# The 32 decay columns of a linear attention, multiplied together with the attention's keys and values

## The chip, the cores and the metric

The kernel runs on one core of a Trainium2 chip. The metric is the device time of one execution in microseconds (us). TensorE multiplies, ScalarE and VectorE read the products out of PSUM, GpSimd (POOL in the profile) takes element-wise work, and SyncE (SP) issues the loads.

## The reference

Two transformer layers on 256 tokens with a context of 256 more (512 in all, width 1024), and then a second block with experts. In each layer one wide weight gives all branches their inputs:

```
(a_q, a_k, a_v, a_g, g_q, g_k, g_v, g_af, g_ab, g_g,
 s_u, s_v, s_g, m_a, m_g, m_s) = jnp.split(h @ p['w_in'], pts, axis=-1)
...
def log_decay(pa, a2, ab):
    z = (pa @ a2 + ab).astype(jnp.float32)
    return heads(jax.nn.log_sigmoid(z) / GLA_GATE_TEMP, GLA_DK)
...
q = rms_norm(pq.reshape(B, N, ATTN_HEADS, ATTN_HEAD_DIM), q_norm)
k = rms_norm(pk.reshape(B, N, ATTN_KV_HEADS, ATTN_HEAD_DIM), k_norm)
```

The attention's keys and values (a_k, a_v) are 256 columns. The linear attention's two decay inputs (g_af, g_ab) are 16 columns each, 32 in all; a small product with a2 widens them to 512 columns, whose log-sigmoid is summed along the tokens.

## The kernel before

Every product is made of three TensorE passes on operands split in two parts: high times high, low times high, high times low. A weight comes in units of 512 rows by 256 columns (tile raw); `split_unit` makes the high part on ScalarE (whi, L97) and the low part on VectorE (wlo, L98). There are three buffers each of raw, whi and wlo. `gemm_T` (L228 to L230) gives products with features on the partitions, `gemm_tok` (L263 to L265) with tokens on the partitions. Their results lie in four PSUM banks that are handed out in turn, two called gm and two called ou; a bank is free for the next product when ScalarE or VectorE has read the last of it. Transposes have two banks of their own (tag tr), the small decay products two others (tag sc).

`branches` calls, for layer 0 once with 512 tokens and for layer 1 twice with 256 tokens, first `gla_proj`, then `attn_kv`. In `gla_proj` come the linear attention's queries (gqps), then the decay columns (gaps, one `gemm_T` over a chunk of 128 columns, of which only 32 are used), copied to pg on ScalarE; four products zps with a2; on ScalarE Abs, Exp and Ln of them (lgt), on VectorE the scans (g); then keys (gkps) and values (gmt, L263 to L265). `attn_kv` multiplies keys and values, copies v, normalises and rotates each tile of 128 keys (`norm_rope`: sq on ScalarE, ms and rsq on VectorE, rs on GpSimd, q on VectorE, ktok on GpSimd), and transposes it (trk).

The order of the instructions on each engine is set by a list scheduler when the program is built, and each engine works through its own list in that order; what a program's text puts first is only an input to it. Layer 1's first half (tokens 0 to 255) also finishes layer 0: the transposes trh, with hTh on ScalarE, hmod on VectorE and hTl on either VectorE or GpSimd, make the context tokens of layer 1's input.

Of the kernel before, what the change touches and what calls it, by code (L numbers as in the profile page):

```python
# [10 lines left out]
F32 = mybir.dt.float32  # L11
# [3 lines left out]
AF = mybir.ActivationFunctionType  # L15
# [29 lines left out]
C_AQ, C_AK, C_AG, C_GQ, C_GK, C_GV = 0, 512, 768, 1280, 1536, 1792  # L45
C_GATE, C_GG, C_SU, C_SV, C_SG = 2304, 2336, 2848, 3360, 3872
# [29 lines left out]
class Builder:  # L76
# [416 lines left out]
        L["kl"] = self.akv.tile([128, 512], F32R, tag="kl", name="kl")  # L493
        L["v"] = self.akv.tile([128, 4, 128], F32, tag="v", name="v")

    def attn_kv(self, t0, t1):
        nc, a, L = self.nc, self.a, self.L
        kh, kl, v = L["kh"], L["kl"], L["v"]
        tts = range(t0 // 128, t1 // 128)
        g = self.gemm_tok(self.chunk(a["w_in"][self.li], C_AK), tts)  # L500
        for tt in tts:
            kt = self.att.tile([128, 512], F32, tag="att2k", name="ktok")[:, :128]
            nc.scalar.activation(v[:, tt], g[tt][:, 128:256], AF.Copy)
            self.norm_rope(g[tt][:, 0:128], 2, 1, tt, kt.rearrange("p (h e) -> p h e", e=64))
            ps = self.ptr.tile([128, 128], F32, tag="tr", name="trk")
            nc.tensor.transpose(ps, kt, self.ident)
            ts = slice(tt * 128, tt * 128 + 128)
            for h in range(2):
                pr, other = slice(64 * h, 64 * h + 64), slice(64 - 64 * h, 128 - 64 * h)
                nc.scalar.activation(kh[pr, h, ts], ps[pr], AF.Copy)  # L510
                nc.vector.tensor_tensor(kl[pr, ts], ps[pr], kh[pr, h, ts].bitcast(F32), op=OP.subtract)
                nc.gpsimd.tensor_copy(kh[other, h, ts], kh[pr, h, ts])
# [135 lines left out]
    def gla_proj(self, t0, t1):  # L648

        nc, a, L = self.nc, self.a, self.L  # L650
        w = a["w_in"][self.li]
        n = t1 - t0
        nq = min(t1, self.nx) - t0
        ts = slice(t0, t1)

        def product(c0, t1, name):
            if c0 not in self.early:
                return self.gemm_T(self.chunk(w, c0), t0, t1, name)
            return self.early.pop(c0)

        def keys():
            for j, ps in enumerate(product(C_GK, t1, "gkps")):
                nc.scalar.activation(L["gk"][:, j, ts], ps, AF.Copy)
            self.tick()

        keys_first = C_GK in self.early
        if nq > 0:
            for j, ps in enumerate(product(C_GQ, t0 + nq, "gqps")):
                nc.scalar.activation(L["gq"][:, j, t0:t0 + nq], ps, AF.Copy, scale=0.125)  # L669
            self.tick()  # L670
        if keys_first:
            keys()
        u = self.chunk(w, C_GATE, 128)
        ps = self.gemm_T(u, t0, t1, "gaps", 128)[0]
        pg = self.tmp.tile([32, 512], F32, tag="tmp", name="pg")[:, :n]
        nc.scalar.activation(pg, ps[:32], AF.Copy)

        logs = []
        for d in range(2):
            t = self.gla.tile([128, 2, 512], F32, tag=("acc", "qin")[d], name="lgt")[:, :, :n]  # L680
            for j in range(2):
                z = self.psc.tile([128, 512], F32, tag="sc", name="zps")[:, :n]
                nc.tensor.matmul(z, L["a2"][:, d * 256 + j * 128:d * 256 + j * 128 + 128], pg, start=True, stop=True)
                ab = L["vT"][:, 24 + 2 * d + j:25 + 2 * d + j]
                nc.scalar.activation(t[:, j], z, AF.Abs, bias=ab)
                nc.vector.tensor_scalar(L["bd"][d][:, j, ts], z, ab, 0.0, op0=OP.add, op1=OP.min)
            logs.append(t)
        for t in logs:
            nc.scalar.activation(t, t, AF.Exp, scale=-1.0)
        for t in logs:  # L690
            nc.scalar.activation(t, t, AF.Ln, bias=1.0)
        for d in range(2):
            b = L["bd"][d][:, :, ts]
            nc.gpsimd.tensor_tensor(b, b, logs[d], op=OP.subtract)
            for j in range(2):
                bj = b[:, j]
                if d == 0:
                    nc.vector.tensor_tensor_scan(bj, self.scan_f[:, :n], bj, 0.0, OP.mult, OP.add)
                else:
                    nc.vector.tensor_tensor_scan(bj[:, ::-1], self.scan_b[:, :n][:, ::-1], bj[:, ::-1], 0.0, OP.mult,  # L700
                                                 OP.add)
        if not keys_first:
            keys()
        tts = range(t0 // 128, t1 // 128)
        for c in range(2):
            g = self.gemm_tok(self.chunk(w, C_GV + 256 * c), tts)
            for tt in tts:
                nc.scalar.activation(L["gv"][:, tt, 256 * c:256 * c + 256], g[tt], AF.Copy)
            self.tick()
# [489 lines left out]
    def branches(self, spans):  # L1199
        with ExitStack() as inner:  # L1200
            self.gla = self.pool("gla", bufs=1, stack=inner, reuse_waits="tile")
            self.att = self.pool("att", bufs=2, stack=inner, reuse_waits="tile")
            self.gla_tiles()
            self.attn_tiles()
            self.alternate = True
            for t0, t1 in spans:
                if t0:
                    self.tick(len(self.pending))
                self.gla_proj(t0, t1)
                self.attn_kv(t0, t1)  # L1210
            self.attn_q()
            self.gla_gate()
            self.alternate = False
            self.sgu_tiles()
            self.gla_core()
            self.attn_gate()
            y = self.L["y_s"] = self.slot.tile([128, 2, 4, self.nx], F32R, tag=self.half, bufs=self.nhalf, name="ysg")
            self.nc.scalar.activation(y[:, 0, 0, 0:1], self.ones, AF.Copy)
            self.attn_core()
            self.sgu_proj()  # L1220
            self.sgu_core()
# [749 lines left out]
```

## Time and profile before

| | us |
|---|---|
| median of 3 runs | 1337.82 |
| lowest, highest | 1335.53, 1343.2 |
| the profiled execution | 1342.17 |
| its span | 1339.8 |
| TensorE busy | 1262.4 |
| VectorE, ScalarE, GpSimd busy | 724.2, 577.9, 334.9 |

The profiled execution took 2.4 us more than its span and 4.3 us more than the median. A busy TensorE in the profile includes modelled ends of its products, so that a short wait can lie inside a busy stretch; the distance between the starts of products tells more.

### The profile page before, as it was taken

Reading aid. Unit: us, or ns where it says so; the run is one execution under the profiler, and the core shown is the slowest. Engines: PE = TensorE matmul, PEld = TensorE weight load, DVE = VectorE, ACT = ScalarE, POOL = GpSimd, SP = SyncE. Lnnn points to the kernel's source line nnn. Section 1 sums busy time; section 2 is a strip of 40 time slices with the busy share of each in tenths; the row PEclk is TensorE's granted clock in tenths of the full one; section 3 lists DMA queues with packets and bytes.
Section 4 is the critical chain, followed back from the end, with each engine's and each line's share of the span. In section 5 each row is a group of like instructions: output and inputs, shape, how many; then the busy total and the mean of one; then the engine's idle time right before and its main releaser. Section 6 shows DMA issues by size and latency. Waiting matters only on the chain.

```text
span 1339.8 us, 22959 instructions
## 1 busy us (share of the span) xinstructions
PE 1262.4 (94%) x8819; PEld 977.2 (73%) x8819; DVE 724.2 (54%) x1428; ACT 577.9 (43%) x1115; POOL 334.9 (25%) x373
## 2 busy tenths in 40 slices
PE   6999999999999999999999999999899989999975
PEld 3789888777777766799989988799898675333311
DVE  2565585775443323378768877646878455111112
ACT  2463454455343222346776554545465333222201
POOL 2237645340001101242246545002124020000000
PEclk9999999999999999999999999999899799999998
DMA  9613222211124676545555546246498546999994
GB/s 320 188 53 110 74 58 79 65 48 48 48 75 132 188 252 221 173 149 167 152 149 157 138 116 186 67 126 193 123 327 252 187 174 257 409 408 409 408 409 185
DMA packets 182165, 243.89 MB, mean 182 GB/s; under 512 B 15284, under 2 KB 154780, under 8 KB 182048
## 3 DMA queue, kind: packets, MB, share of 16 engines
q1 hardware_dynamic: 182048, 242.35, 54.9%
q8 instruction: 71, 1.16, 0.4%
q14 instruction: 46, 0.38, 0.1%
HBM read 241.27 MB, written 1.05 MB: 181 GB/s over the span
## 4 chain that ended last, share of the span: by engine, by line
PE 65%; DMA 15%; DVE 8%; ACT 4%; issue 3%; POOL 2%; SPq 1%; ACTq 0%; DVEq 0%; POOLq 0%
DMA gu<-w_up 7%; PE mgps L228 5%; PE mgps L230 5%; PE mgps L229 5%; PE gmt L263 4%; PE gmt L264 4%; PE gmt L265 4%; PE gups L1737 3%; DVE wlo L98 2%; DMA dn<-w_down 2%; DMA raw<-w_in 2%; PE brps L228 2%; PE brps L229 2%; PE brps L230 2%; PE aops L631 2%
## 5 line engine op out<-in xcount | busy, mean ns | idle before, releaser
L98 DVE TENSOR_TENSOR wlo<-raw,whi 128x1024 fp32r<-128x1024 f32 (+1 forms) x202 | 253.5, 1261 | 156.7 <-ACT whi L97 153.8
L97 ACT ACTIVATE whi<-raw 128x1024 fp32r<-128x1024 f32 (+1 forms) x216 | 212.5, 993 | 199.3 <-PE mgps L229 41.8
L264 PE MATMUL gmt<-wlo,hTh 128*128 128x256 f32 x480 | 138.0, 288 | 2.5 <-DVE wlo L98 2.5
L263 PE MATMUL gmt<-whi,hTh 128*128 128x256 f32 x480 | 137.3, 287 | 2.1 <-DVE a L587 0.9
L265 PE MATMUL gmt<-whi,hTl 128*128 128x256 f32 x480 | 137.3, 286 | 0.0
L228 PE MATMUL mgps<-hTh,whi 128*128 128x512 f32 (+1 forms) x384 | 132.0, 345 | 0.0
L229 PE MATMUL mgps<-hTl,whi 128*128 128x512 f32 (+1 forms) x384 | 130.6, 340 | 0.0
L230 PE MATMUL mgps<-hTh,wlo 128*128 128x512 f32 (+1 forms) x384 | 130.4, 342 | 0.0
L957 POOL TENSOR_TENSOR msum<-msum,tanh 128x512 f32<-128x512 f32 (+1 forms) x32 | 36.8, 1154 | 329.7 <-DVE tanh L956 310.2
L1737 PE MATMUL gups<-gu,xw 128*64 128x512 f32 (+1 forms) x512 | 97.5, 603 | 8.4 <-DMA gu<-w_up 8.4
L264 PEld LDWEIGHTS gmt<-wlo,hTh 128*128 128x128 f32 x480 | 92.6, 193 | 5.9 <-DVE wlo L98 2.9
L263 PEld LDWEIGHTS gmt<-whi,hTh 128*128 128x128 f32 x480 | 92.5, 193 | 3.9 <-ACT g L669 1.1
L265 PEld LDWEIGHTS gmt<-whi,hTl 128*128 128x128 f32 x480 | 92.7, 193 | 2.3 <-issue 2.2
L228 PEld LDWEIGHTS mgps<-hTh,whi 128*128 128x128 f32 x384 | 72.6, 189 | 12.9 <-issue 5.0
L230 PEld LDWEIGHTS mgps<-hTh,wlo 128*128 128x128 f32 x384 | 72.5, 189 | 10.2 <-issue 2.5
L229 PEld LDWEIGHTS mgps<-hTl,whi 128*128 128x128 f32 x384 | 72.7, 189 | 9.0 <-issue 2.0
L1737 PEld LDWEIGHTS gups<-gu,xw 128*64 128x64 f32 (+1 forms) x512 | 25.3, 124 | 62.0 <-issue 60.0
L203 POOL TENSOR_TENSOR frs<-rsq,mhalf 128x1 f32<-128x1 f32 x2 | 1.1, 549 | 234.7 <-DVE frs L1911 234.7
L1769 DVE SCALAR_TENSOR_TENSOR eth<-eth,gups 128x256 f32<-128x256 f32 x12 | 5.1, 421 | 99.8 <-ACT eth L1768 99.8
L1792 PE MATMUL dnps<-dn,hm 128*64 128x512 f32 (+1 forms) x256 | 52.2, 599 | 6.2 <-DMA dn<-w_down 6.0
L264 PE MATMUL gmt<-wlo,mm 128*128 128x256 f32 x192 | 54.5, 285 | 0.6 <-DVE wlo L98 0.6
L263 PE MATMUL gmt<-whi,mm 128*128 128x256 f32 x192 | 54.1, 285 | 0.0
(559 smaller groups left out, 3109.2 us busy)
## 6 DMA issues: line engine op xcount, KB each, us to landing
raw<-w_in SPq DMA_DIRECT2D x132, 512.0 KB
gu<-w_gate SPq DMA_DIRECT2D x64, 512.0 KB
gu<-w_up SPq DMA_DIRECT2D x64, 512.0 KB
dn<-w_down SPq DMA_DIRECT2D x28, 1024.0 KB
adar<-w_ada SPq DMA_DIRECT2D x32, 512.0 KB
raw<-w_out SPq DMA_DIRECT2D x32, 512.0 KB
adaw<-w_ada SPq DMA_DIRECT2D x16, 512.0 KB
raw<-w_in SPq DMA_DIRECT2D x32, 256.0 KB
```

Of the source, the lines that this page charges most:

```text
L97: nc.scalar.activation(hi, x, AF.Copy)
L98: return (eng or nc.vector).tensor_tensor(lo, x, hi.bitcast(F32), op=OP.subtract).ins
L228: nc.tensor.matmul(ps, wh, xh, start=(u == 0 and k == 0), stop=False)
L229: nc.tensor.matmul(ps, wh, xl, start=False, stop=False)
L230: nc.tensor.matmul(ps, wl, xh, start=False, stop=(u == len(acts) - 1 and k == 3))
L263: nc.tensor.matmul(out[tt], xh, hi[:, j, :n], start=first, stop=False, skip_group_check=True)
L264: nc.tensor.matmul(out[tt], xh, lo[:, j, :n], start=False, stop=False, skip_group_check=True)
L265: nc.tensor.matmul(out[tt], xl, hi[:, j, :n], start=False, stop=last, skip_group_check=True)
L631: nc.tensor.matmul(ops[halves[g], r], v[:, keys[0] // 128 + k, 64 * g:64 * g + 64], pts[g][:, k], start=(k == 0), stop=(k == nkc - 1), ski ...
L957: nc.gpsimd.tensor_tensor(sums[c, j], sums[c, j], ts[j], op=OP.add)
L1737: mm = nc.tensor.matmul(u["ps"][pr], u["x"][:, k, pr], u["gu"][ei][k // 4][:, :, k % 4], start=(k == 0), stop=(k == 7), skip_group_check=T ...
L1792: mm = nc.tensor.matmul(ps[pr], hm[:, f, pr], dns[ei][:, f, 512 * hf:512 * hf + 512], start=(f == 0), stop=(f == 1), skip_group_check=True ...
```

## The change

The chunk of 128 decay columns is no longer loaded and multiplied by itself. A new function loads 288 columns, 256 of keys and values and 32 of decay, in three units of 384, 384 and 256 rows (864, 864 and 576 elements in a partition), and multiplies them as tokens by features into one bank for each tile of 128 tokens (kvps). ScalarE copies the 32 decay columns of each tile (gt), TensorE transposes them (trg), and ScalarE copies the result to pg. `attn_kv` no longer multiplies: it takes the same banks, and is called in `gla_proj` ahead of the decay's further work.

```
-    def attn_kv(self, t0, t1):
+    def keys_values_gate(self, tts):
+
+
+        nc, w = self.nc, self.a["w_in"][self.li]
+        out = {tt: self.bank([128, 512], "kvps")[:, :288] for tt in tts}
+        for k0 in range(0, 8, 3):
+            nk = min(3, 8 - k0)
+            raw, hi, lo = (t.rearrange("p a n -> p (a n)")[:, :288 * nk].rearrange("p (a n) -> p a n", n=288)
+                           for t in self.unit_tiles())
+            for cs, c0, n in ((slice(0, 256), C_AK, 256), (slice(256, 288), C_GATE, 32)):
+                nc.sync.dma_start(raw[:, :, cs], w[128 * k0:128 * (k0 + nk), c0:c0 + n].rearrange(
+                    "(a p) n -> p a n", p=128))
+            self.split_unit(hi, lo, raw)
+            for tt in tts:
+                ts = slice(tt * 128, tt * 128 + 128)
+                for j in range(nk):
+                    k = k0 + j
+                    xh, xl = self.hTh[:, k, ts], self.hTl[:, k, ts]
+                    nc.tensor.matmul(out[tt], xh, hi[:, j], start=(k == 0), stop=False)
+                    nc.tensor.matmul(out[tt], xh, lo[:, j], start=False, stop=False)
+                    nc.tensor.matmul(out[tt], xl, hi[:, j], start=False, stop=(k == 7))
+        return out
+
+    def attn_kv(self, tts, g):
         nc, a, L = self.nc, self.a, self.L
         kh, kl, v = L["kh"], L["kl"], L["v"]
-        tts = range(t0 // 128, t1 // 128)
-        g = self.gemm_tok(self.chunk(a["w_in"][self.li], C_AK), tts)
...
-        u = self.chunk(w, C_GATE, 128)
-        ps = self.gemm_T(u, t0, t1, "gaps", 128)[0]
+        tts = range(t0 // 128, t1 // 128)
+        g = self.keys_values_gate(tts)
+        gt = self.tmp.tile([128, 4, 32], F32, tag="tmp", name="gt")
+        tp = self.ptr.tile([128, 512], F32, tag="tr", name="trg")[:32, :n]
+        for i, tt in enumerate(tts):
+            nc.scalar.activation(gt[:, i], g[tt][:, 256:288], AF.Copy)
+            nc.tensor.transpose(tp[:, 128 * i:128 * i + 128], gt[:, i], self.ident)
         pg = self.tmp.tile([32, 512], F32, tag="tmp", name="pg")[:, :n]
-        nc.scalar.activation(pg, ps[:32], AF.Copy)
+        nc.scalar.activation(pg, tp, AF.Copy)
+        self.attn_kv(tts, g)
...
                 self.gla_proj(t0, t1)
-                self.attn_kv(t0, t1)
```

The scheduler's lists change with it. In layer 0, this stands on ScalarE before, where the decay columns' copy pg is made (whi are the splits of the next weights, br and sgr belong to another branch's constants):

```order
L97 ACTIVATE whi_613<-raw_612 128x1024
L97 ACTIVATE whi_721<-raw_720 128x1024
L676 ACTIVATE pg_576<-gaps_551 32x512
L377 ACTIVATE br_511<-wsum_513 1x512
L382 ACTIVATE sgr_521<-sgr_516 128x512
L685 ACTIVATE lgt_578<-zps_579,vT_136 128x512
```

And this stands there now:

```order
L97 ACTIVATE whi_801<-raw_800 128x1024
...
L699 ACTIVATE gt_660<-kvps_542 128x32
L524 ACTIVATE v_534<-kvps_542 128x128
L97 ACTIVATE whi_909<-raw_908 128x1024
L702 ACTIVATE pg_670<-trg_661 32x512
L560 ACTIVATE sq_674<-kvps_539 128x128
L712 ACTIVATE lgt_766<-zps_767,vT_136 128x512
```

Four copies gt and four copies v, one of each for a tile, and a split (whi_909) have come ahead of pg, and the normalisation (sq) has come between the decay's steps. On TensorE the same place reads now, from the last product of the 288 columns on (zps are the products with a2, gmt_806 is the first bank of the linear attention's values; it is the bank in which kvps_539 lay):

```order
L516 MATMUL kvps_542<-whi_630,hTl_108 128x288
L700 MATMUL trg_661<-ident_74,gt_660 32x128 x4
L710 MATMUL zps_767<-pg_670,a2_477 128x512
L710 MATMUL zps_771<-pg_670,a2_477 128x512
L710 MATMUL zps_776<-pg_670,a2_477 128x512
L263 MATMUL gmt_806<-whi_795,hTh_107 128x256
```

Before, 29 products of the values stood between gaps and the first zps there, and more between one zps and the next; none stand between kvps and the third zps now.

In layer 1's first half TensorE had this before around the first two decay products (gkps are the linear attention's keys):

```order
L230 MATMUL gkps_6245<-hTh_5329,wlo_6241 128x256
L683 MATMUL zps_6206<-pg_6203,a2_3751 128x256
L683 MATMUL zps_6210<-pg_6203,a2_3751 128x256
L228 MATMUL gkps_6246<-hTh_5329,whi_6234 128x256
L229 MATMUL gkps_6246<-hTl_5330,whi_6234 128x256
```

It has this now:

```order
L516 MATMUL kvps_6151<-whi_6203,hTl_5314 128x288
L700 MATMUL trg_6222<-ident_74,gt_6221 32x128 x2
L710 MATMUL zps_6282<-pg_6227,a2_3735 128x256
L710 MATMUL zps_6286<-pg_6227,a2_3735 128x256
L228 MATMUL gkps_6321<-hTh_5313,whi_6310 128x256
```

And ScalarE has this now, from the split that needs the buffer of the third unit of the 288 columns (whi_6385) on:

```order
L97 ACTIVATE whi_6385<-raw_6384 128x1024
L699 ACTIVATE gt_6221<-kvps_6150 128x32
L699 ACTIVATE gt_6221<-kvps_6151 128x32
L524 ACTIVATE v_6074<-kvps_6150 128x128
L524 ACTIVATE v_6074<-kvps_6151 128x128
L702 ACTIVATE pg_6227<-trg_6222 32x256
L560 ACTIVATE sq_6231<-kvps_6150 128x128
L476 ACTIVATE hTh_5313<-trh_6139,mb_3783,ms_3782 128x256
```

Between kvps and zps there were the first bank of keys and several transposes before; now there is nothing. gkps_6321 takes the bank of kvps_6150, so it follows that tile's normalisation, and on GpSimd hTl of the same trh stands ahead of that normalisation's rs.

## Rows read from the trace of the kernel before

**Rows 1.** The page's part 1, busy time of each engine.
```profile
PE 1262.4 (94%) x8819; PEld 977.2 (73%) x8819; DVE 724.2 (54%) x1428; ACT 577.9 (43%) x1115; POOL 334.9 (25%) x373
```

**Rows 2.** Waits of TensorE between 50 and 125 us: total, times, longest.
```profile
PE early L239 <- DVE hTl L481: 1.5, 1, 1.5
```

**Rows 3.** TensorE in layer 0: the decay columns' stage; then timeline (start, duration).
```profile
56.39:61.95 5.56, 5.56 (x24) 1.00 0.67 186
...
63.45 0.28 PE L265 MATMUL gmt<-whi,hTl 128*128 128x256 f32 x1
...
65.97 0.28 PE L265 MATMUL gmt<-whi,hTl 128*128 128x256 f32 x1
...
67.65 1.02 PE L683 MATMUL zps<-pg,a 32*128 32x512 f32 x2
```

**Rows 4.** Timeline of ScalarE in layer 0.
```profile
61.93 1.06 ACT L97 ACTIVATE whi<-raw 128x1024 fp32r<-128x1024 f32 x1 [1.61 <-PE gaps L229]
62.89 0.57 ACT L676 ACTIVATE pg<-gaps 32x512 f32<-32x512 f32 x1
...
68.71 0.69 ACT L685 ACTIVATE lgt<-zps,vT 128x512 f32<-128x512 f32 x1 [0.27 <-PE zps L683]
...
73.64 1.04 ACT L689 ACTIVATE lgt<-lgt 128x1024 f32<-128x1024 f32 x1
...
75.73 1.28 ACT L691 ACT_TABLE_LOAD   x1
77.03 1.06 ACT L691 ACTIVATE lgt<-lgt 128x1024 f32<-128x1024 f32 x1
```

**Rows 5.** Timelines of GpSimd and VectorE in layer 0, the decay's sums.
```profile
78.16 2.41 POOL L694 TENSOR_TENSOR g<-g,lgt 128x1024 f32<-128x1024 f32 x1 [25.92 <-ACT lgt L691]
...
80.60 2.34 DVE L698 TENSOR_TENSOR_SCAN g<-ku,g 128x512 f32<-128x512 uint8 x2 [0.61 <-POOL g L694]
82.86 0.67 DVE L741 TENSOR_TENSOR kh<-g 128x512 f32<-128x512 f32 x1
83.44 0.75 DVE L786 TENSOR_TENSOR qlv<-g 128x256 f32<-128x256 f32 x2
```

**Rows 6.** Timelines of GpSimd and VectorE in layer 0, a key tile's normalisation.
```profile
101.87 0.71 POOL L203 TENSOR_TENSOR rs<-rsq,mhalf 128x2 f32<-128x2 f32 x1 [6.77 <-DVE rsq L202]
...
102.61 0.29 DVE L546 TENSOR_TENSOR q<-gmt,rs 128x128 f32<-128x128 f32 x1 [0.82 <-POOL rs L203]
```

**Rows 7.** Timeline of TensorE in layer 1's first half.
```profile
631.29 1.13 PE L683 MATMUL zps<-pg,a 32*128 32x256 f32 x4
...
635.32 1.04 PE L470 MATMUL trh<-ident,xc 128*128 128x128 f32 x8
637.24 0.66 PE L263 MATMUL gmt<-whi,hTh 128*128 128x256 f32 x2 [0.88 <-ACT g L669]
```

**Rows 8.** Timelines of ScalarE, VectorE and GpSimd there.
```profile
629.92 0.55 ACT L476 ACTIVATE hTh<-trh,mb,ms 128x256 fp32r<-128x256 f32 x1
...
630.46 0.36 ACT L676 ACTIVATE pg<-gaps 32x256 f32<-32x256 f32 x1
...
631.71 0.54 DVE L477 TENSOR_SCALAR hmod<-trh,ms,mb 128x256 f32<-128x256 f32 x1
...
633.07 1.30 POOL L481 TENSOR_TENSOR hTl<-hmod,hTh 128x512 fp32r<-128x512 f32 x1 [8.34 <-DVE sp L1256]
```

**Rows 9.** TensorE after its wait in layer 1's second half; a stage's us, busy, clock, DMA.
```profile
686.28 0.39 PE L264 MATMUL gmt<-wlo,hTh 128*128 128x256 f32 x1 [2.18 <-DVE wlo L98]
...
687.47 0.41 PE L264 MATMUL gmt<-wlo,hTh 128*128 128x256 f32 x1
...
690.66 0.38 PE L264 MATMUL gmt<-wlo,hTh 128*128 128x256 f32 x1
...
688.00:689.00 1.00, 1.00 (x7) 0.50 1.00 341
```

**Rows 10.** Waits of ScalarE between 600 and 760 us: total, times, longest.
```profile
ACT whi L97 <- DMA raw<-w_in: 5.3, 5, 2.0
```

More of the change, by code (lines that the diff above doesn't have):

```diff
@@ L703, in gla_proj @@
             keys()
-        tts = range(t0 // 128, t1 // 128)
         for c in range(2):
```

## The prediction

> **What bounds the kernel now.** I read the busy times first: TensorE works 1262.4 us of the span, VectorE 724.2 [rows 1]. Then the waits in layer 0, where the decay columns are first multiplied: from 50 to 125 us TensorE waits once, 1.5 us, for hTl on VectorE [rows 2]. The starts of its products agree: they follow each other without a hole. So in layer 0 a product removed gives its full time back, and an instruction that TensorE must wait for costs its full wait; work taken off ScalarE, VectorE and the loads gives nothing there. In layer 1 there are waits before the change too, 0.88 us for a bank behind the transposes trh [rows 7] and 2.18 us for a split [rows 9].
>
> **What is removed on TensorE.** The 24 products gaps of layer 0 take 5.56 us, 0.232 each at 512 columns [rows 3]. At 256 columns 21 steps from 63.45 to 65.97 us make 0.120 each [rows 3]. A product of 288 columns is not in the trace; on the line between the two it takes 0.120 + 32/256 x 0.112 = 0.134 us (bounds: 0.120 and 0.232, but the line is steady between close neighbours, so I take it). Layer 0: 5.56 for gaps plus 96 x 0.120 = 11.5 for keys and values were there, 96 x 0.134 = 12.9 come: 4.2 us saved. Each half of layer 1: 24 x 0.120 + 48 x 0.120 = 8.7 were there, 48 x 0.134 = 6.4 come: 2.3 saved. Together 8.8 us. Eight transposes trg of 32 columns come; eight of 128 take 1.04 [rows 7], so 0.13 each at most, 1.0 us in all. Without any wait the change would give 7.8 us.
>
> The splits shrink by 768 elements in a partition for each call, 0.8 us on ScalarE by the 1.06 for 1024 [rows 4]. I count that as nothing, because TensorE's own work covers it.
>
> **What is added: a longer way to the decay, with nothing beside it.** The order shown ahead says what TensorE has in its list meanwhile.
>
> Layer 0, first wait. The last product of the 288 columns must end (0.2 us), then ScalarE makes gt and v, the split whi_909 (1.06) and only then pg (0.57) [rows 4]; trg runs beside the split. A gt of 32 columns is not in the trace; it lies between nothing and the 0.57 of pg, I take 0.25, nearer the low end because it reads a sixteenth of the columns. With hand-offs of 0.1 that is 2.2 us from the last product to the first zps. Before, 29 products of values lay there.
>
> Second wait. The third zps needs the bank of the first, which VectorE empties after ScalarE's Abs. Count from the first zps, Z: Abs starts at Z+1.06 and VectorE follows 0.72 later for 0.75 us (68.71 against 67.65 [rows 3, 4]; the VectorE step is taken as long as the qlv pair [rows 5]), so Z+2.6. TensorE is ready at Z+2.0: 0.55 us.
>
> Third wait. The transpose trk of the second key tile now stands 42 products behind; TensorE gets there at Z + 3.1 (three zps) + 0.55 + 42 x 0.120 + 1.1 (fourth zps, first trk) = Z+9.8. Its tile's last addition stands on VectorE behind both scans. Those need Abs of the second zps (to Z+2.8), Exp 1.04, a table load 1.28, Ln 1.06 [rows 4], GpSimd's subtraction 2.41, scans 2.34, kh 0.67, qlv 0.75 [rows 5], and the addition, 0.29 like q [rows 6]: Z+12.6. TensorE waits 2.8 us. The fourth tile's trk waits about 0.5 more, counted in the same way behind GpSimd's second subtraction (bounds: none, and the 2.8 of the one before). Ahead of all this the first split has 864 elements instead of 512 and stands before hmod on VectorE, in the chain to the one wait of [rows 2]: 352 of 1024 elements at 1.06 are 0.4 more.
>
> Layer 0 in sum: 2.2 + 0.55 + 2.8 + 0.5 + 0.4 = 6.4 lost (trg inside), 4.2 saved: 2.2 us longer.
>
> Layer 1, first half. Count from the last product of the 288 columns, E. ScalarE's next split, whi_6385, needs the buffer that this product has just read, so it starts at E+0.1 and takes 1.06; gt follows, trg, pg 0.36 [rows 8]; zps starts at E+2.4 and two of them take 1.06 (631.29 to the next product at 632.35; the row has 1.13 with the modelled end [rows 7]). The keys' product gkps_6321 then needs the bank of kvps_6150. That is free after sq (not in the rows, taken as long as q), hTh 0.55, hmod 0.54, hTl on GpSimd 1.30 [rows 8], rs 0.71, q 0.29 [rows 6]: 3.7 us, from pg's end at E+2.4 to E+6.1. Of these 6.1 us TensorE works 1.06 on zps: 5.0 lost (trg inside). Behind the keys three groups of transposes trh stand together; the second needs the bank of the last trk, whose release stands on ScalarE behind a split and an hTh and on VectorE behind a split and an hmod; the copies of gq that free the next bank come last. A split 1.06, hTh 0.55, VectorE's part of the split taken as long (1.06), hmod 0.54, four transposes 0.5, hTh 0.55, a copy taken as long as pg (0.36) sum to 4.6; the split starts about 0.3 ahead of the first trh's end, so TensorE stands there for 4.3 us, with two trh, 1.0, as work: 3.3 lost, where 0.88 were lost before [rows 7]. This half: 5.0 + 2.4 - 2.3 = 5.1 us longer.
>
> Layer 1, second half. Here trg and zps stand between the keys' products, and no new wait falls before TensorE. 2.3 saved, 0.25 for trg. The wait of 2.18 us for a low part [rows 9] comes again behind the same scans, and another split now stands beside it; I take half of it more, 1.1 (bounds: none, and 2.2). This half: 0.9 us shorter.
>
> Sum before the clock: 2.2 + 5.1 - 0.9 = 6.4 us longer.
>
> **The clock.** After the wait of 2.18 us TensorE's granted clock is 0.50, that is 1.2 instead of 2.4 GHz, between 688 and 689 us [rows 9]; from 687.47 to 690.66 us 15 steps take 0.213 each instead of 0.120: 1.4 us. After the wait of 0.88 [rows 7] the steps stay at 0.120. Four of the new waits, 2.2, 2.8, 5.0 and 3.3 us, are as long as the one that was followed by a fall; but zps runs inside some. I take two falls, 2.8 us; bounds none and four (5.6). The Trainium skill (TensorE: Matmul & The Clock Gate, section A second HAM failure mode: psum-queue depth-cycling) says that short pauses between groups of products that cycle through PSUM banks make the clock swing between its levels. The trace agrees in one case of two; by that rule all four waits would be followed by a fall, the second rival below.
>
> Sum: 6.4 + 2.8 = 9.2 us longer. The profiled execution of 1342.2 would become 1351.4; against the median, 4.3 lower, 1337.8 + 9.2 = 1347.0.
>
> **The rivals.** I call a difference of over 0.5% (6.7 us) a change, about what a measurement of this kernel can tell from none.
>
> Waits without falls of the clock: 6.4 longer, 1344.2, just inside 0.5%. For it: the 0.88 wait had none, and zps keeps TensorE busy inside two of the waits.
>
> All four waits with a fall: 6.4 + 5.6 = 12.0 longer, 1349.8. For it the one wait of 2.18 us, against it again the 0.88 and zps.
>
> The other side: ScalarE and VectorE reach the new steps in time, no wait opens, and 7.8 us are saved: 1330.0. It decides at the first zps of layer 0: if pg is done within 0.3 us of the last trg there. For it speaks that ScalarE is busy 577.9 us of the span only [rows 1]; against it the order, in which a split that needs 1.06 us stands between.
>
> Half of it: layer 0 as forecast without its third wait, layer 1's bank chain shorter by GpSimd's 1.30 and the second trh wait gone: 9.2 - 2.8 - 1.3 - 2.4 - 2.8 = 0 longer, 1337.8.
>
> Worse: the 32 decay columns come in pieces of 128 bytes and the first unit of each of the three stretches lands late. ScalarE waited for loads of w_in five times, 2.0 us at the longest [rows 10], and TensorE for none of them; three such waits on TensorE give 9.2 + 6.0 = 15.2 longer, 1353. The Trainium skill (DMA: Bandwidth & Descriptors, Specifications) wants 512 bytes or more for line rate; no row here has such pieces of a weight, and by that rule this case would be the likelier one.
>
> **How the numbers follow.** Waits and one to three falls (7.8 to 10.6 longer): 0.40, the forecast, 1347.0. Waits without falls 0.23; four falls 0.10; half 0.11; other side 0.07; worse 0.09. Slower by over 0.5%: the forecast, four falls and the worse case, and 0.02 of the case without falls, 0.61. Faster by over 0.5%: 0.07. Within: 0.32. The range reaches from a little under the half case, 1336, to the worse one, 1353; outside lie the other side and about a tenth more.
>
> **What would show it.** In the profile after: kvps steps of 0.134 us; in layer 0 a hole of some 2 us between trg and zps, and one of some 3 us before the second trk; in layer 1's first half some 6 us from the last kvps to gkps with two zps inside, ended by q; then some 4 us around trh, ended by g; a granted clock of 0.50 behind two of them. Wrong would be: no wait of TensorE for pg, q or ktok over 1 us, or kvps steps near 0.2.

## The result and the profile after

The change makes the kernel slower: 1354.53 us median of 4 runs (1353.72 to 1356.33) against 1336.67 of 4 runs of before (1333.11 to 1343.2), ratio 1.0129 [1.0105, 1.0153], 17.9 us. Timed once more beside other kernels it was 1357.75 of 6 runs against 1336.73 of 15, ratio 1.0160 [1.0126, 1.0194]. The direction was forecast; 1354.53 lies outside the range, and the loss is twice the 9.2 us forecast.

The page of the changed kernel, busy time of TensorE and the granted clock in 40 slices of the span: TensorE works 3.7 us more than in [rows 1] although it counts 64 instructions fewer.

```profile
PE 1266.1 (93%) x8755; PEld 980.7 (72%) x8755; DVE 720.2 (53%) x1425; ACT 579.0 (43%) x1120; POOL 340.1 (25%) x373
...
PEclk9989999999999999999898989999999989999988
```

The same row of before:

```profile
PEclk9999999999999999999999999999899799999998
```

In the change the slices of 34 us that begin at 68, 643, 711 and 779 us have an 8 where before has a 9.

The waits of TensorE in the changed kernel (total, times, longest), from 0 to 60, 60 to 140 and 600 to 660 us. The first answers to [rows 2], the last stretch to [rows 7]:

```profile
PE early L239 <- POOL hTl L481: 2.6, 1, 2.6
...
PE zps L710 <- ACT pg L702: 1.3, 1, 1.3
PE zps L710 <- DVE g L713: 0.7, 1, 0.7
...
PE gkps L228 <- DVE sp L1284: 3.2, 1, 3.2
PE trh L470 <- DVE kl L532: 2.7, 1, 2.7
...
PE gmt L263 <- ACT g L690: 0.5, 1, 0.5
```

In layer 1's first half the waits came where they were forecast. As the profile names them they are 1.2 + 0.5 + 3.2 = 4.9 us from the last kvps to gkps (forecast 5.0 lost), and 2.7 + 0.2 (a third wait, for hmod) + 0.5 = 3.4 around trh (3.3). Counted as the forecast counted, as distance less work, they are a little longer: 5.4 (6.5 us less 1.1 on zps) and 4.2 (5.2 us from the end of the first trh to gmt, less 1.0 on the other two). The timeline of TensorE shows the same places, in layer 0 first:

```profile
47.80 1.07 PE L238 MATMUL early<-hTh,whi 128*128 128x512 f32 x4
...
57.96 0.38 PE L514 MATMUL kvps<-whi,hTh 128*128 128x288 f32 x1
...
73.06 0.29 PE L516 MATMUL kvps<-whi,hTl 128*128 128x288 f32 x1
...
75.21 1.98 PE L710 MATMUL zps<-pg,a 32*128 32x512 f32 x4 [1.28 <-ACT pg L702]
77.89 1.49 PE L710 MATMUL zps<-pg,a 32*128 32x512 f32 x2 [0.71 <-DVE g L713]
79.31 0.58 PE L263 MATMUL gmt<-whi,hTh 128*128 128x256 f32 x1
...
141.36 0.60 PE L551 MATMUL trq<-ident,a 128*128 128x128 f32 x4
...
635.80 0.29 PE L516 MATMUL kvps<-whi,hTl 128*128 128x288 f32 x1
...
636.47 0.29 PE L516 MATMUL kvps<-whi,hTl 128*128 128x288 f32 x1
638.00 0.39 PE L700 MATMUL trg<-ident,gt 128*32 128x128 f32 x2 [1.23 <-ACT gt L699]
638.85 1.13 PE L710 MATMUL zps<-pg,a 32*128 32x256 f32 x4 [0.46 <-ACT pg L702]
643.14 0.55 PE L228 MATMUL gkps<-hTh,whi 128*128 128x256 f32 x1 [3.16 <-DVE sp L1284]
...
648.40 0.35 PE L527 MATMUL trk<-ident,ktok 128*128 128x128 f32 x1
...
654.89 0.64 PE L470 MATMUL trh<-ident,xc 128*128 128x128 f32 x4 [2.72 <-DVE kl L532]
```

Five steps of kvps from 635.80 to 636.47 are 0.134 each, as worked out. From the end of the last kvps (636.47 + 0.13) to gkps pass 6.5 us (forecast E + 6.1). But the 24 products from gkps at 643.14 to trk at 648.40 take 5.3 us, where 0.120 each would be 2.9; and the 17 products from 79.31 to the next zps at 83.24 take 3.9 instead of 2.0. Stretches of the changed kernel (length, TensorE busy, granted clock, DMA share and GB/s at the end):

```profile
79.00:88.00 9.00, 9.00 (x33) 6.96 (x33) 6.58 (x12) 5.51 (x10) 7.62 (x10) 0.50 0.01 3
642.00:648.00 6.00, 4.86 (x23) 4.89 (x24) 4.28 (x24) 0.00 (x0) 3.28 (x12) 0.50 0.13 47
656.00:662.00 6.00, 5.53 (x26) 5.13 (x25) 2.65 (x6) 5.24 (x12) 1.28 (x1) 0.50 0.21 61
728.00:733.00 5.00, 5.00 (x24) 5.00 (x25) 4.49 (x6) 1.52 (x3) 4.05 (x7) 0.50 0.75 207
```

So TensorE works at 1.2 instead of 2.4 GHz behind the waits, by the steps of its products for 3 us (from 51.5) to 10 us (from 78.9) each time, where the prediction took two falls of 3 us; two others lie from 805 to 812 and from 839 to 843 us. One comparison goes the other way in these two executions: from 1046 to 1059 us the clock was 0.50 before and 1.00 in the change, which is one reason why the two spans differ by 14.8 us only.

Where the loss arises I read from starts of the same work in both traces. The executions do not reach layer 0 at the same time, so I count from the last products ahead of the wait for hTl, 47.80 in the change and 48.81 before:

```profile
48.81 1.07 PE L238 MATMUL early<-hTh,whi 128*128 128x512 f32 x4
...
137.05 0.60 PE L530 MATMUL trq<-ident,a 128*128 128x128 f32 x4
```

To layer 0's first trq pass 88.2 us before, 93.6 in the change and 93.3 in the second execution of it that was profiled: 5.3 and 5.1 more. Of the 5.3, 2.6 are there at the first product behind the wait (57.96, which answers to 56.39 in [rows 3]). From trq to layer 1's first gqps, in work that the change does not touch, before took 481.0, the change 482.0 and 484.3. From there to layer 1's last agps, its projections, before took 111.2, the change 122.7 and 118.6: 11.5 and 7.3 more. From there to the last brps, the merge of the branches, before took 202.2, the change 205.5 and 204.7: 3.3 and 2.5 more, again in work that the change does not touch. The four parts sum to 21.1 and 18.3 us; the medians differ by 17.9 and 21.0.

### The profile page after: what moved, and what is told of

The parts are those of the page before. It is cut to its first block, busy times and chain, and to the rows that moved or that the text cites. A ratio compares the mean times of both kernels' runs of the same rounds, so it can differ in the third digit from the quotient of the medians.

```text
span 1354.6 us, 22857 instructions
## 1 busy us (share of the span) xinstructions
PE 1266.1 (93%) x8755; PEld 980.7 (72%) x8755; DVE 720.2 (53%) x1425; ACT 579.0 (43%) x1120; POOL 340.1 (25%) x373
## 4 chain that ended last, share of the span: by engine, by line
PE 66%; DMA 17%; DVE 6%; ACT 4%; POOL 3%; issue 2%; SPq 0%; ACTq 0%; DVEq 0%; POOLq 0%
DMA gu<-w_up 9%; PE gmt L263 5%; PE mgps L228 5%; PE gmt L264 5%; PE gmt L265 5%; PE mgps L230 4%; PE mgps L229 4%; DMA dn<-w_down 3%; PE brps L228 2%; PE brps L229 2%; PE aops L652 2%; PE brps L230 2%; DVE wlo L98 2%; PE gups L1762 2%; ACT whi L97 2%
## 5 line engine op out<-in xcount | busy, mean ns | idle before, releaser
L98 DVE TENSOR_TENSOR wlo<-raw,whi 128x1024 fp32r<-128x1024 f32 (+3 forms) x199 | 248.4, 1254 | 194.6 <-ACT whi L97 190.7
L97 ACT ACTIVATE whi<-raw 128x1024 fp32r<-128x1024 f32 (+3 forms) x213 | 210.2, 996 | 206.6 <-PE mgps L229 42.1
L263 PE MATMUL gmt<-whi,hTh 128*128 128x256 f32 x416 | 121.3, 292 | 1.4 <-DVE a L608 0.9
L264 PE MATMUL gmt<-wlo,hTh 128*128 128x256 f32 x416 | 120.8, 290 | 1.4 <-DVE wlo L98 1.3
L265 PE MATMUL gmt<-whi,hTl 128*128 128x256 f32 x416 | 120.5, 290 | 0.0
L1762 PE MATMUL gups<-gu,xw 128*64 128x512 f32 (+1 forms) x512 | 100.5, 621 | 7.2 <-DMA gu<-w_up 7.2
L263 PEld LDWEIGHTS gmt<-whi,hTh 128*128 128x128 f32 x416 | 82.2, 198 | 3.6 <-ACT lgt L716 1.1
L264 PEld LDWEIGHTS gmt<-wlo,hTh 128*128 128x128 f32 x416 | 82.3, 198 | 2.4 <-DVE wlo L98 1.8
L265 PEld LDWEIGHTS gmt<-whi,hTl 128*128 128x128 f32 x416 | 82.2, 198 | 0.3 <-issue 0.3
```

Source lines behind the costliest of these rows:

```text
L97: nc.scalar.activation(hi, x, AF.Copy)
L98: return (eng or nc.vector).tensor_tensor(lo, x, hi.bitcast(F32), op=OP.subtract).ins
L263: nc.tensor.matmul(out[tt], xh, hi[:, j, :n], start=first, stop=False, skip_group_check=True)
L264: nc.tensor.matmul(out[tt], xh, lo[:, j, :n], start=False, stop=False, skip_group_check=True)
L265: nc.tensor.matmul(out[tt], xl, hi[:, j, :n], start=False, stop=last, skip_group_check=True)
L1762: mm = nc.tensor.matmul(u["ps"][pr], u["x"][:, k, pr], u["gu"][ei][k // 4][:, :, k % 4], start=(k == 0), stop=(k == 7), skip_group_check=T ...
```

## The experiments

Theory: the packed products are a gain by themselves. The loss is the order around them: banks of kvps held until the normalisation has read them, a decay chain with nothing beside it, and falls of the granted clock behind these waits. Rivals were that packing itself costs (small pieces of loads, larger splits), and that moving the normalisation ahead of the scans costs whatever the products are. Differences are of medians against before on the same chip:

| kernel | median, us | longer than before | ratio |
|---|---|---|---|
| change_again | 1357.75 | 21.0 | 1.0160 [1.0126, 1.0194] |
| l0_only | 1348.99 | 10.0 | 1.0082 [1.0057, 1.0108] |
| l1_only | 1346.17 | 7.2 | 1.0057 [1.0036, 1.0078] |
| order_alone | 1344.03 | 5.0 | 1.0038 [1.0022, 1.0055] |
| late_norm | 1348.04 | 9.0 | 1.0072 [1.0045, 1.0098] |
| small_first | 1362.84 | 23.9 | 1.0187 [1.0158, 1.0215] |
| late_small | 1343.83 | 4.9 | 1.0033 [1.0013, 1.0052] |
| l0_late | 1336.57 | -2.4 | 0.9987 [0.9967, 1.0007] |
| busy_zps | 1352.43 | 13.5 | 1.0111 [1.0075, 1.0146] |
| busy_full | 1352.26 | 15.5 | 1.0111 [1.0086, 1.0136] |
| busy_late | 1354.69 | 18.0 | 1.0114 [1.0085, 1.0143] |
| late_keys | 1344.63 | 7.9 | 1.0050 [1.0031, 1.0069] |
| bank_step | 1353.79 | 14.3 | 1.0120 [1.0089, 1.0150] |
| l0_only_bank | 1346.29 | 6.8 | 1.0047 [1.0025, 1.0070] |
| late_small_bank | 1341.22 | 1.7 | 1.0023 [1.0000, 1.0046] |

**The change again**, without an edit.

> The change itself once more, beside the kernels that are compared with it. Every theory: 16 to 18 us longer than before; falls of the granted clock in the same places of layer 1, each 5 to 7 us long.

It was 21.0 longer, above the 16 to 18 expected; half clock from 643 to 650 and from 657 to 663 us again, but not behind the first agps, where the first execution had it (728 to 733). The wait in front of that agps was 1.8 us in both: some falls repeat, others don't.

**One layer alone.** The packed part stands under a condition on the layer, the other layer keeps the code of before:

```
+        if self.li in (0,):        # l1_only: (1,)
+            g = self.keys_values_gate(tts)
...
+        else:
+            u = self.chunk(w, C_GATE, 128)
+            ps = self.gemm_T(u, t0, t1, "gaps", 128)[0]
...
+                if self.li not in (0,):
+                    self.attn_kv(range(t0 // 128, t1 // 128))
```

> Layer 0 packs the 288 columns as the change does, layer 1 works as before. Theory (waits that the new order opens, and falls of the granted clock behind them): layer 1 begins about 5 us late, as in the trace of the change (+5.4), with waits of 1.3 us for pg and 0.7 us for g and a granted clock of 0.50 for some 10 us behind them; layer 1 adds nothing, so 5 us longer in all (2 to 8). Rival (layer 0's saving of 4.2 us on products is real at the end and layer 1 alone costs): 3 to 4 us shorter.

> Layer 1 packs, layer 0 works as before. Theory: waits of about 3.2 us before gkps and 2.7 us before the second trh again, each with a granted clock of 0.50 for 5 to 7 us behind it, and 11 to 13 us longer in all. Rival (half of the loss stems from layer 0's changed lists and buffers carried into layer 1): 7 us longer or less.

The two parts (10.0 and 7.2) add up to the change. But layer 1 alone costs what the rival said, and layer 0 alone costs more than either said, although in layer 0 itself the execution loses the 5.0 us of the theory (its fall there lasts 4 us, not 10): 4.5 more go in layer 1's projections and 2.0 behind the last agps, in unchanged code. That pointed at the lists further on (below).

**The order alone.** Products of before, `attn_kv` called where the change has it:

```
         nc.scalar.activation(pg, ps[:32], AF.Copy)
+        self.attn_kv(t0, t1)
...
                 self.gla_proj(t0, t1)
-                self.attn_kv(t0, t1)
```

> Products, loads and splits of before (a chunk of 128 decay columns, 256 columns of keys and values), but keys and values are multiplied and normalised ahead of the decay's further work, where the change has them. Theory: 48 products (layer 1) or 96 (layer 0) of keys and values stand between gaps and zps, and the next keys' product takes a bank of the queries, so that neither the wait for pg nor the one of 3.2 us before gkps comes; at most the second trh or trk waits, 1 to 3 us; 0 to 4 us longer in all. Rival (the early normalisation itself, its work on ScalarE, VectorE and GpSimd ahead of the scans, makes the loss): 10 us longer or more.

It lies between the two: 5.0. Layer 0 loses 0.4, but layer 1's projections take 6.9 more. Waits of TensorE from 600 to 660 us in order_alone:

```profile
PE trh L470 <- DVE kl L511: 2.8, 1, 2.8
PE trk L506 <- DVE ktok L559: 1.5, 1, 1.5
```

Falls of the clock stand behind both. So multiplying and normalising early is enough to open a wait at trh, with the products of before; late_norm, next, has that wait without it.

**Banks given back at once.** Keys are copied out beside the values; the normalisation reads the copy at its old place:

```
...
-        self.attn_kv(tts, g)
+        kc = L["gg"][:, :, 0:128]
+        for tt in tts:
+            nc.scalar.activation(L["v"][:, tt], g[tt][:, 128:256], AF.Copy)
+            nc.scalar.activation(kc[:, tt], g[tt][:, 0:128], AF.Copy)
+        self.kc = kc
...
                 self.gla_proj(t0, t1)
+                self.attn_kv(range(t0 // 128, t1 // 128), self.kc)
```

> 288 columns packed in both layers, but keys are copied out of their bank on ScalarE right away, beside the values, and normalised from the copy at the old place, after the linear attention's values. Theory: the bank of kvps is free 0.5 us after its products, so the wait of 3.2 us before gkps and the one of 2.7 us behind trk go, with the fall behind each (2.3 and 2.2 us); the wait for gt, trg and pg stays; 8 to 10 us shorter than the change, 1344 to 1347. Rival (the packed products, their smaller pieces of loads and their larger splits cost by themselves): within 3 us of the change, 1352 or more.

Half of the loss goes: 9.0. Waits of TensorE from 600 to 660 us in late_norm:

```profile
PE trh L470 <- DVE sp L1289: 2.8, 1, 2.8
PE trg L699 <- ACT gt L698: 1.2, 1, 1.2
PE gkps L228 <- ACT g L689: 0.5, 1, 0.5
```

The wait of 3.2 before gkps is now 0.5, so it was the held bank. The wait at trh stays, against the theory: no trk stands ahead of it here, so it does not need trk's release. By the order I put it down to three groups of trh one behind the other, each waiting for the copies of the group before; only late_keys, below, bears on that.

**The first split.**

```
-        for k0 in range(0, 8, 3):
-            nk = min(3, 8 - k0)
+        for k0, nk in ((0, 2), (2, 3), (5, 3)):
```

> The change with the 288 columns in units of 256, 384 and 384 rows instead of 384, 384 and 256, so that the first split has 576 elements and not 864; GpSimd's list has hTl ahead of the mask cast ku again, as before the change. Theory (the larger first split moved the cast ahead of hTl, and the cast waits for its load): the wait for hTl at 50 us falls from 2.6 to about 1.5 us, the granted clock of 0.50 behind it goes, and layer 0 is 1.6 to 2.8 us shorter; the rest stays, 15 us longer than before. Rival (the cast's place is chance and the wait comes from the split itself): the wait stays above 2 us, time as the change.

> The kernel late_norm with units of 256, 384 and 384 rows. Theory: late_norm (9 longer than before) less the same 1.6 to 2.8 us at hTl, so 6 to 8 longer than before; the wait of 2.8 us at trh in layer 1 stays. Rival (waits elsewhere take it up): 9 or more.

> Only layer 0 packs the 288 columns, with the small first unit and with keys copied out of their banks at once and normalised at the old place; layer 1 as before. Theory: TensorE has the values' products beside the decay's chain again, so the saving of 4.2 us less 1.0 for trg remains, less a wait of about 1.6 us for the second trk: 0 to 3 us shorter than before at layer 0's end and in all. Rival (packing costs by itself): 4 us longer or more.

In all three the wait for hTl is 1.6 and no half clock stands behind it, as the theory said. In the change GpSimd's list has the cast ku ahead of hTl, and ku waits for its load:

```profile
49.60 0.62 POOL L289 CAST ku<-kf 128x384 uint8<-128x384 f32 x1 [4.83 <-DMA kf<-k_masks]
50.19 1.26 POOL L481 TENSOR_TENSOR hTl<-hmod,hTh 128x512 fp32r<-128x512 f32 x1
```

But small_first is slower still, 23.9 longer where 15 was expected. In layer 0 a product gmt then waited 3.8 us for a q of the normalisation, which frees a bank of kvps, and a fall stands behind it:

```profile
PE gmt L263 <- DVE q L566: 3.8, 1, 3.8
```

With the banks given back (late_small) layer 0 takes 86.3 us, 2.0 less than before, and late_small is 4.9 longer than before in all, a little better than expected. l0_late, packing layer 0 alone in this way, takes 86.3 there too (48.30 to 134.56), as do late_keys and late_small_bank, and is the fastest kernel of the study, 2.4 us under before, which the interval can't tell from none:

```profile
134.56 0.60 PE L554 MATMUL trq<-ident,a 128*128 128x128 f32 x4
```

l0_only and l0_late differ by 12 us with the same packed products and the same 32-column loads (and units of another cut). In layer 0, packing by itself is no loss.

**Work for TensorE inside the waits.** busy_zps repeats a decay product; busy_full and busy_late put products of 128 rows there (busy_late has 0 in place of 12):

```
+                    for _ in range(7 if self.li and not t0 and d == 0 and j else 1):   # busy_zps
...
+        self.last_kv = mm.ins                                                   # busy_full
...
+                fill = (12, 26)[j] if self.li and not t0 and d == 0 else 0
+                if fill:
+                    with self.tc.issue_after(self.last_kv if j == 0 else zi.ins):
+                        for _ in range(fill):
+                            nc.tensor.matmul(z, self.hTh[:, 0, 0:128], self.hTh[:, 1, 0:256], start=True, stop=True)
```

> The change with the second decay product of layer 1's first half issued seven times into the same bank (six repeats of 0.53 us, 3.2 us), so that TensorE works in the wait for the bank of kvps; the output is unchanged. Theory (a fall of the granted clock follows an idle stretch of TensorE): the wait of 3.2 us before gkps shrinks to about nothing, gkps starts at the same distance from the last kvps (6.5 us), and its steps take 0.120 instead of 0.213 us, 2.3 us shorter in that stretch; the fall behind trh stays. Rival (the fall has another cause, or filler does not count): steps of 0.213 us behind it all the same, time as the change or up to 3 us longer.

> The change with filler products of the granted clock's usual kind (128 rows, 256 columns, 0.120 us each, written to the banks of zps and overwritten by it) in the two waits of layer 1's first half: 12 between the last kvps and trg, 26 between the first zps and the second, ahead of gkps. The output is unchanged. The repeats of zps before (32 rows) did not keep the clock. Theory (the fall follows a stretch in which TensorE has too little of such work): no granted clock of 0.50 before trh, gkps starts at the same distance from the last kvps (6.5 us), its 24 steps that took 0.213 take 0.120, so 2.3 us shorter in that stretch; the fall behind trh may stay. Rival (the falls come at certain times of the run or from power drawn before, whatever TensorE does in the wait): steps of 0.213 us all the same, time as the change.

> The same with the second filler alone, 26 products between the first zps and the second; the 2.2 us from the last kvps to zps stay without work. Theory: it tells which of the two waits the fall belongs to. In the repeats of zps the clock fell 3.2 us behind the last kvps, so the first wait alone is followed by a fall and this kernel has one of 5 us or more, with no gain. Rival: the wait of 3.2 us is the one, and the fall is gone as with both fillers, 2.3 us shorter.

A row of the timeline of TensorE in busy_zps, and then a stretch of it (columns as above):

```profile
641.88 6.59 PE L711 MATMUL zps<-pg,a 32*128 32x256 f32 x16 [0.46 <-ACT pg L702]
```

```profile
643.00:652.00 9.00, 9.00 (x30) 7.26 (x30) 6.17 (x31) 0.28 (x1) 5.16 (x13) 0.50 0.31 99
```

From 641.88 on TensorE was busy without a hole, and from 642.5 to 652.8 us it worked at half clock all the same: the rival held for this filler. The wait of 3.2 us is not needed for the fall; the 1.2 + 0.5 us ahead of zps were still there. Rows of the timeline of TensorE in busy_full, and then two stretches of it:

```profile
638.89 3.37 PE L715 MATMUL zps<-hTh 128*128 128x256 f32 x26
...
642.81 0.39 PE L228 MATMUL gkps<-hTh,whi 128*128 128x256 f32 x1
...
645.80 0.27 PE L528 MATMUL trk<-ident,ktok 128*128 128x128 f32 x1
```

```profile
642.00:652.00 10.00, 7.49 (x59) 6.79 (x57) 7.58 (x28) 3.68 (x8) 5.09 (x15) 1.00 0.13 36
652.00:658.00 6.00, 5.11 (x23) 4.60 (x24) 3.93 (x8) 4.70 (x12) 0.64 (x2) 0.50 0.44 111
```

With 128-row filler in both waits the first fall is gone: gkps to trk takes 3.0 us instead of 5.3. The second, behind trh, where no filler stands, remains. In busy_late, with the second filler alone, the clock fell inside the filler itself, and was back when gkps came; I had expected a longer fall. A row of its timeline and a stretch of it:

```profile
639.50 4.85 PE L715 MATMUL zps<-hTh 128*128 128x256 f32 x26
```

```profile
641.00:643.00 2.00, 2.00 (x11) 2.00 (x11) 1.76 (x10) 0.28 (x1) 1.05 (x2) 0.50 1.01 314
```

So in both kernels that leave the first wait open a fall follows it, whatever stands behind: from 640.2 to 643.7 us over the 128-row filler, from 642.5 to 652.8 over the decay products. Each is one execution. In time the three are 3 to 8 us under change_again, but their intervals overlap with that of the change's first timing, so the trace shows the gain of this one fall, the medians don't.

**Groups of trh apart.** late_small with `keys()` called ahead of the decay's logarithms.

> The kernel late_small with the linear attention's keys put ahead of the decay's logarithms in the program, so that in layer 1 one group of trh stands between trg and zps and the keys' products stand whole ahead of the third zps. Theory (waits open where TensorE has nothing else in its list): the wait of 1.5 us for pg falls under 0.7 and the one of 2.9 us at trh under 2; 1 to 3 us shorter than late_small, 2 to 4 longer than before. Rival (the group order only moves the wait): as late_small, 5 longer.

The wait at trh fell from 2.9 to 1.5, as the theory said, but the one for pg stayed at 1.5, and in time the rival was right: it is 7.9 longer, not better than late_small (the intervals overlap).

**The turn of the banks.** One line ahead of layer 1, in three kernels:

```
             self.li, self.L, self.nx, self.half = 1, self.layers[1], 256, "half"
+            self.n_bank += 1
```

> The change with the turn of the four PSUM banks moved on by one ahead of layer 1 (layer 0 takes four banks for kvps where it took three for gaps, keys and values, which turned the order round). The lists up to layer 1's projections stay the same but for the banks' names; behind them the scheduler puts 192 products mgps between the last ups and the last tro, as before the change, where the change has 144. Theory (a part of the loss that no step of the prediction held is the merge's products moved out of the waits of the linear attention's core): from the last agps to the last brps it takes 2 us less than before, as in the kernels with that list (-1.6 to -2.0), where the change takes 2.5 to 3.3 more; 3 to 5 us shorter than the change in all, 12 to 14 longer than before. Rival (the waits in the core are paid wherever the products stand): as the change, 17 to 21 longer.

> l0_only with the same turn of the banks; the list behind the projections becomes that of before too. Theory: l0_only was 11 longer though its layer 0 ends only 3 to 5 late; 3 to 5 of it are the merge's products, so 6 to 8 longer. Rival: 11 longer.

> late_small (4.9 longer than before) with the same turn of the banks. Theory: 2 to 4 us shorter than late_small, 1 to 3 longer than before; layer 1's first half still has the wait of 2.9 us at trh with a fall behind it, while layer 0 ends 2 to 3 early. Rival: as late_small.

Starts of the last agps and the last brps in change_again and then in bank_step:

```profile
745.53 0.28 PE L230 MATMUL agps<-hTh,wlo 128*128 128x256 f32 x1
...
950.24 0.28 PE L230 MATMUL brps<-yat,wlo 128*128 128x256 f32 x1
```

```profile
743.22 0.28 PE L230 MATMUL agps<-hTh,wlo 128*128 128x256 f32 x1
...
943.60 0.28 PE L230 MATMUL brps<-yat,wlo 128*128 128x256 f32 x1
```

204.7 us there, 200.4 here, 1.8 under before as expected: 4.3 us in a stretch whose code is the same. The waits for qlv in the linear attention's core, 3.7 us in change_again, are 0.4 in bank_step. In all bank_step is 14.3 longer, between the 12 to 14 expected and the 17.9 of the change; its interval overlaps with the change's. l0_only_bank (6.8) and late_small_bank (1.7) lie inside their expectations, and their intervals overlap with those of l0_only and late_small too. The traces of layer 1's unchanged code say it more plainly: in l0_only its projections and merge took 4.5 and 2.0 us more than before, in l0_only_bank each took 0.6 less.

## Why the prediction was wrong in size

**Products and prices: right.** kvps steps 0.134; the small copies gt took 0.18 to 0.20 in layer 0, 0.25 was taken.

**Layer 1's first half, waits: right.** 4.9 and 3.4 us of waits for 5.0 and 3.3 forecast (5.4 and 4.2 in the forecast's own count). The chain to gkps went as written (ScalarE, GpSimd and VectorE in the changed kernel):

```profile
636.80 1.06 ACT L97 ACTIVATE whi<-raw 128x1024 fp32r<-128x1024 f32 x1
...
638.43 0.37 ACT L702 ACTIVATE pg<-trg 32x256 f32<-32x256 f32 x1
...
640.10 1.26 POOL L481 TENSOR_TENSOR hTl<-hmod,hTh 128x512 fp32r<-128x512 f32 x1 [9.01 <-DVE sp L1281]
641.32 0.70 POOL L203 TENSOR_TENSOR rs<-rsq,mhalf 128x2 f32<-128x2 f32 x1
...
642.70 0.29 DVE L567 TENSOR_TENSOR q<-kvps,rs 128x128 f32<-128x128 f32 x1
```

The split ahead of pg, hTl on GpSimd ahead of rs, then q, which frees the bank. late_norm shows the bank as the cause. The forecast's reason for the wait at trh, the bank of the last trk, was not shown: late_norm has the wait without a trk ahead of it.

**Layer 1's second half: partly wrong.** The forecast's "no new wait falls before TensorE" did not hold: it waited 0.8 us for trq and 1.8 for agps, where before has 0.9 in all before agps. The wait for a low part was 1.3, not the 3.3 of the forecast, so in sum the error is small.

**Layer 0: about right before the clock, by luck in part.** The first wait was 2.0 from the last kvps to zps (2.2), the second 0.71 (0.55). The hTl term was called 0.4 and cost 2.6 up to the first kvps, half clock included. It held VectorE's longer split only, but the scheduler also put ku ahead of hTl on GpSimd, and the clock fell behind the wait. The third wait of 2.8 us for the second trk did not come in this execution, because TensorE arrived late: between 79 and 88 us it worked at half clock. In change_again the fall was shorter and the wait came, 1.1 us, with 0.8 more for kl. Wait and fall stood in for each other (93.6 and 93.3 us), and the sum had both as separate terms.

**The clock: the step that failed.** "I take two falls, 2.8 us", at 1.4 each, from one fall of 3 us in [rows 9]. In the two layers' projections there were five (from 51.5, 78, 641, 655 and 727 us). The gkps products lost 2.4, the 23 gmt products behind trh 2.3 (5.1 us for 2.8), the agps products 2.7. The longer one in layer 0 lost about 4.4: 1.9 on 17 products, 1.0 on the fourth zps and 1.5 on 15 more products. A fall's length was the wrong thing to take from a single row.

What half clock cost in a whole stretch can be estimated: the time that TensorE was busy at half clock, in slices of a quarter of a microsecond, times 0.44, the share that a step loses when it takes 0.213 instead of 0.120. What before lost in the same stretch is taken off (nothing in layer 0, 1.5 us in layer 1's projections).

| longer than before, us | change | change_again | forecast |
|---|---|---|---|
| layer 0 | 5.3 | 5.1 | |
| of that, half clock | 5.8 | 3.0 | |
| the rest | -0.5 | 2.1 | 2.2 |
| layer 1's projections | 11.5 | 7.3 | |
| of that, half clock | 6.2 | 2.7 | |
| the rest | 5.3 | 4.6 | 4.2 |

So products and waits together cost 4.8 and 6.7 us where the forecast had 6.4, and half clock 12.0 and 5.7 where it had 2.8. The mechanism was right, and the clock's term was two to four times too small. The mean granted clock of all executions points the same way: 0.963 to 0.972 in the ten of the change, 0.981 on average in the fifteen of before beside change_again.

The Trainium skill (TensorE: Matmul & The Clock Gate, section A second HAM failure mode: psum-queue depth-cycling) describes a clock that swings between its levels because TensorE pauses often between groups of products that cycle through PSUM banks. The trace agrees for the long waits: those of 2.6 us for hTl, of 4.9 before gkps and of 2.7 at trh were followed by a fall in both executions, the 1.8 before agps in one of them. Of the rivals, the case with four falls, 12.0 longer, was the nearest by its mechanism; the worse case, 15.2, came nearer in number, but for a reason, late loads, that did not show.

**A term that was missing: the lists behind the change.** Nothing in the sum held the stretch from agps to brps. Layer 0 now takes four banks in place of three, the turn of the banks is reversed from there on, and the scheduler's list in layer 1's core has 144 products of the merge where 192 were, with less beside the waits for qlv. bank_step puts the turn back and the stretch is 4.3 shorter. By the estimate above this term is the clock's again: half clock cost 4.2 and 3.8 us in that stretch in the change's two executions, 1.5 before and nothing in bank_step, which has 0.4 us of waits for qlv. The turn alone does not decide the list (l0_late has the old one without it).

**The rivals.** Loads in 128-byte pieces were not late: ScalarE's waits for w_in from 600 to 760 us were two, 2.6 us in all (four in change_again, 5.0; five before, 5.3), and TensorE waited for none there. The other side (a gain) needs pg within 0.3 us of trg; it was late by the split. But a gain of 2.0 us in layer 0 does exist in four traces, with the small first unit and the banks given back at once.

What stays open: the shares of waits and clock rest on two traces, and the falls vary from execution to execution; what took 3.3 us more between trq and layer 1 in change_again, where the half clock differs by 0.3; what decides the scheduler's list beside the turn of the banks; and a version of layer 1 that packs without its waits was not found.

## What to carry to other kernels

When a product takes over a bank's content for two users, the bank lives until the slower user has read it: copy that part out, or every product behind it in the bank's turn waits for a normalisation. Count a new wait of TensorE with the slowed products that may stand behind it, from several rows and not from one (here the 1.8 us before agps had a fall behind it in one execution, and 2.3 us there in bank_step had none), and don't add a later wait that such a fall would hide. Where a scheduler sets the lists, compare them behind the change too: a changed number of banks can move unrelated work.

## What the hardware showed

TensorE at work did not by itself keep its clock. Behind the same wait of 1.2 + 0.5 us a fall to 0.50 came among eight decay products of 32 rows and lasted 10 us, into the products behind them (busy_zps), and it came among 26 products of 128 rows and lasted under 4 us (busy_late). With twelve products of 128 rows in the 1.2 us as well, the clock stayed at 1.00 until the wait at trh (busy_full).

Small steps of GpSimd and VectorE stretch beside each other. In the changed kernel four rotations took 0.88 us beside short steps of VectorE and 3.35 while its scans ran, and one step of 4 columns on VectorE took 1.25 while hTl ran on GpSimd and 0.16 behind it:

```profile
78.53 0.88 POOL L578 TENSOR_TENSOR q<-q,rs 128x32 f32<-128x32 f32 x4
...
84.19 3.35 POOL L578 TENSOR_TENSOR q<-q,rs 128x32 f32<-128x32 f32 x4
...
640.13 1.25 DVE L1284 TENSOR_TENSOR sp<-sp 128x4 f32<-128x4 f32 x1
...
641.62 0.16 DVE L1284 TENSOR_TENSOR sp<-sp 128x4 f32<-128x4 f32 x1
```

The Trainium skill (SBUF — State Buffer, section SBUF: two separate sides) says that GpSimd and a VectorE step with two inputs in SBUF share one pair of ports, and that the one that starts first holds it for its whole instruction; the trace agrees, as the slow step of VectorE began 0.03 us behind the start of hTl and ended 0.02 behind its end.
